# Conditioning and gate rows in four column groups of TensorE, three tiles in the first round, and moved loads, in a one-core layer kernel

## The chip, the cores and the metric

One core of one Trainium2 chip runs the whole kernel. The metric is the device time of one execution in microseconds (us). In the trace PE is TensorE (matrix products), DVE is VectorE, ACT is ScalarE, POOL is GpSimd, and SP is SyncE, which here only issues DMAs. A DMA is issued by the engine whose queue it stands in (SP, ACT or POOL) and lands later by itself. An engine carries out its own instructions in order.

## The reference

One layer of a hybrid backbone for 256 prompt tokens and 2048 latent tokens, D_MODEL = 1024, all in float32:

```python
shift, scale, gate = jnp.split(jax.nn.silu(cond) @ w_mod + b_mod, 3, axis=-1)
xm = _rmsnorm(x, norm_g) * (1.0 + scale[:, None]) + shift[:, None]
(q, k, v, g_na, u, g_lru, c_b, c_c, c_h, g_conv,
 m_na, m_lru, m_conv) = jnp.split(xm @ w_in, SPLIT_IDX, axis=-1)
...
merged = (jax.nn.sigmoid(m_na) * ((o_na * jax.nn.silu(g_na)) @ w_br_na)
          + jax.nn.sigmoid(m_lru) * (((h_f + h_b) * jax.nn.silu(g_lru)) @ w_br_lru)
          + jax.nn.sigmoid(m_conv) * ((o_conv * jax.nn.silu(g_conv)) @ w_br_conv))
x = x + gate[:, None] * (merged @ w_out)
```

o_na is attention with 8 heads of 64: the prompt attends to itself, and each latent token to a window of its 32 x 64 grid (with a bias per head) and to 256 cached keys, in one softmax. h_f and h_b come from two gated linear recurrences, o_conv from short convolutions. cond has two rows, one for the prompt and one for the latents. A last RMSNorm gives the outputs; the prompt's keys, values and final states are outputs too.

## The kernel before

Tokens are cut into chunks: chunk 0 is the prompt (256 tokens), chunks 1 to 4 are 512 latent tokens each. Phase A (`ORDA`) takes chunks 1, 2, 0, and phase B (`ORDB`) chunks 3 and 4. In each phase the input projection goes through tiles of 128 columns of `w_in`: tile m is loaded by `load_w` (two DMAs `wraw` from SP, split into a high part `whi` on ACT and a low part `wlo` on POOL, both rounded), and `w_in_chunk` (L153) multiplies it with a chunk of the normalised input, which is split likewise (`xh`, `xl`). Each product is three passes (high by high, low by high, high by low) over 8 blocks of 128 rows, so one tile of a 512-token chunk is 24 matmuls of 512 columns. `dense` runs a list of such tiles over the chunks of its phase; a `Side` is a generator that `dense` ticks at a given rate, so that recurrences, gate rows and attention stand between the matmuls of the projection. The order of instructions on each engine comes out of this program order and of when buffers of the tile pools come free; a scheduler fixes it before the run.

What the change touches, in program order:

- **Conditioning** (L249 to L269). In eight steps kk a DMA from SP brings 128 rows of `w_mod` (1 MB, tiles `wmxhB`, `wmxlB`, `wm`), and four float32 matmuls (L254) with two weight columns (`sc`, the two conditioning rows) and 512 moving columns add into four PSUM banks `pm`. Then rows 0 and 1 of each bank are copied (`mrow`), transposed (`pmt`, L265) and made into `shft` and `amod`, which the first normalised chunk needs.
- **First round.** Tiles 16 and 17 run over the chunks while the next chunk is prepared.
- **Gate rows** (`gate_rows`, L382 to L399). The last 1024 columns of `w_mod`, needed only at the very end, in 16 float32 matmuls (L396) that stand one by one between projection tiles, each behind its own 256 KB load `wg` (two buffers).
- **Keys of the prompt** (`key_out`, L346). Each of four key tiles is copied by ACT (`kc`, L376) and transposed (`ktr`); the last pair of transposes stands right behind the last product of its tile.
- **Attention** (`latent_steps`, `latent_units`). For phase A group 0, for phase B groups 1, 2 and 3 of each head: jobs (g, h). POOL's queue issues the loads: keys `kd` and `ck` and values `vb` per head, queries `qs` (512 KB) and gate `sg` per job, and the bias `bt` per head and kind (kind 1 serves groups 1 and 2, kind 2 serves group 3; two buffers). PE computes scores `sc` and `sl` (L583, L587), DVE adds `bt` and takes the maximum (L590), ACT exponentiates, DVE normalises (`p`, L598), PE transposes `p` (`t`, L613) and multiplies with the values (`o`, L628). `p_first` is the `p` of the first block of phase B.
- **Branch products** (L922 to L946). For each chunk and branch the operand `zr` is loaded (SP, L927), split into `zh` and `zl`, and multiplied with branch weights into `pb` (L937); the results are scaled by `tg` (the tanh values that tiles 40 to 63 stored in `d_sig`), added on POOL (L944) and stored to `d_mrg` by ACT's queue.
- **Output projection** (from L950). `mr` loads merged rows from `d_mrg` (L958), which are split into `mh` and `ml` and multiplied into `po` (L986). The first 128 rows are already there (`m0h`, `m0l`).

## Time and profile before

| what | before |
|---|---|
| runs | 2567.19, 2556.35, 2554.89 us; median 2556.35 us |
| the profiled execution | 2558.7 us, span 2556.9 us |
| PE busy | 2492.1 us (97% of the span), 13192 records |
| DVE, ACT, POOL busy | 43%, 38%, 34% |
| mean granted clock of PE | 0.989 |
| DMA | 360.84 MB, mean 141 GB/s |

The profiled execution lies 2.3 us above the median of the runs, and 1.8 us of it lie outside the span. PE is busy nearly throughout; the other engines and the DMA matter where PE waits for them.

### The profile page before, as it was taken

What the parts mean: (1) busy time and instruction counts of PE and PEld (TensorE: products, weight loads), DVE (VectorE), ACT (ScalarE), POOL (GpSimd) and SP (SyncE); (2) the same over time, 40 slices, a digit from 0 to 9 for tenths busy, and PEclk for the clock granted to TensorE, in tenths of its full rate; (3) what the DMA queues carried; (4) which work ended last, traced back from release to release, by engine and by line L of the source; (5) the groups of instructions that cost most, each with busy time, mean ns of one, the idle gap of its engine ahead of it and who ended that gap; (6) DMA issues with size and microseconds to landing.
All of it is one profiled execution on the core that took longest, in us unless ns stands there. A gap on an engine that the chain in (4) does not pass through costs nothing. (4 is left out here: it accounts for less than half of the span.)

```text
span 2556.9 us, 35325 instructions
## 1 busy us (share of the span) xinstructions
PE 2492.1 (97%) x13192; PEld 2060.1 (81%) x13192; DVE 1096.7 (43%) x2329; ACT 976.5 (38%) x1849; POOL 878.3 (34%) x757
## 2 busy tenths in 40 slices
PE   8999999999999999999999998999999999999998
PEld 3887678888878888888888887778877788888887
DVE  5101244555223332314877873455544144333433
ACT  4311444344223334335766563445544311011221
POOL 2411223233542321332444444333331313335642
PEclk9999999999999999999999999999999999999999
DMA  7335552322743543345553326546552475555542
GB/s 280 110 91 153 160 132 84 75 58 65 185 118 107 155 146 136 101 133 117 185 162 120 118 87 183 170 142 179 170 145 82 148 239 181 181 161 189 176 137 83
DMA packets 248812, 360.84 MB, mean 141 GB/s; under 512 B 88761, under 2 KB 124729, under 8 KB 247617
## 3 DMA queue, kind: packets, MB, share of 16 engines
q1 hardware_dynamic: 147360, 227.20, 29.5%
q0 software_dynamic: 47920, 64.26, 9.0%
q10 hardware_dynamic: 53360, 67.13, 7.9%
q8 instruction: 104, 1.70, 0.3%
q14 instruction: 68, 0.55, 0.1%
HBM read 248.10 MB, written 110.11 MB: 140 GB/s over the span
## 5 line engine op out<-in xcount | busy, mean ns | idle before, releaser
L153 PE MATMUL ps<-xh,whi 128*128 128x512 f32 (+1 forms) x2400 | 899.8, 375 | 0.0
L153 PE MATMUL ps<-xl,whi 128*128 128x512 f32 (+1 forms) x2400 | 889.4, 371 | 2.1 <-DVE xl L56 1.6
L153 PE MATMUL ps<-xh,wlo 128*128 128x512 f32 (+1 forms) x2400 | 888.8, 370 | 0.0
L153 PEld LDWEIGHTS ps<-xh,whi 128*128 128x128 f32 x2400 | 455.9, 190 | 91.9 <-ACT qo L367 5.2
L56 POOL TENSOR_TENSOR wlo<-wraw,whi 128x512 fp32r<-128x512 f32 x240 | 336.2, 1418 | 550.9 <-ACT whi L55 491.3
L153 PEld LDWEIGHTS ps<-xl,whi 128*128 128x128 f32 x2400 | 456.0, 190 | 78.5 <-POOL xl L56 2.5
L153 PEld LDWEIGHTS ps<-xh,wlo 128*128 128x128 f32 x2400 | 455.3, 190 | 77.9
L55 ACT CAST whi<-wraw 128x512 fp32r<-128x512 f32 x240 | 144.9, 616 | 298.8 <-PE ps L153 168.4
L937 PE MATMUL pb<-zh,wbh 128*128 128x512 f32 (+1 forms) x480 | 179.0, 373 | 4.5 <-ACT zh L55 4.5
L937 PE MATMUL pb<-zl,wbh 128*128 128x512 f32 (+1 forms) x480 | 179.2, 373 | 0.0
L937 PE MATMUL pb<-zh,wbl 128*128 128x512 f32 (+1 forms) x480 | 179.1, 373 | 0.0
L167 ACT ACTIVATE evm<-ps 128x512 f32<-128x512 f32 (+1 forms) x120 | 66.4, 553 | 283.8 <-PE ps L153 282.9
L944 POOL TENSOR_TENSOR tg<-tg,tg 128x512 f32<-128x512 f32 (+1 forms) x80 | 97.0, 1223 | 188.2 <-DVE tg L940 183.4
L588 DVE TENSOR_SCALAR_CACHE_REDUCE p<-sc 128x256 f32<-128x256 f32 x127 | 53.2, 422 | 207.6 <-PE sc L583 206.9
L940 DVE SCALAR_TENSOR_TENSOR tg<-tg,pb 128x512 f32<-128x512 f32 (+1 forms) x120 | 74.9, 631 | 156.5 <-PE pb L937 146.6
L596 ACT ACTIVATE p<-p,ast 128x736 f32<-128x736 f32 (+2 forms) x127 | 109.6, 863 | 41.6 <-DVE ast L595 39.6
L444 DVE SCALAR_TENSOR_TENSOR uf<-ut,pk,uf 128x512 f32<-128x512 f32 (+1 forms) x120 | 104.2, 868 | 31.4 <-ACT uf L441 29.5
L613 PE MATMUL t<-ident,p 128*128 128x128 f32 x698 | 98.7, 275 | 18.9 <-DVE p L598 17.3
L475 POOL TENSOR_TENSOR sq<-sq,ea 128x512 f32<-128x512 f32 (+1 forms) x40 | 61.9, 1549 | 153.5 <-ACT sq L468 94.7
L55 ACT CAST zh<-zr 128x512 fp32r<-128x512 f32 (+1 forms) x60 | 30.5, 575 | 212.3 <-PE pb L937 99.9
L617 ACT COPY pT<-t 128x512 f32<-128x512 f32 (+3 forms) x256 | 95.3, 407 | 37.4 <-PE t L613 37.4
L937 PEld LDWEIGHTS pb<-zh,wbh 128*128 128x128 f32 x480 | 90.8, 189 | 22.3 <-ACT zh L55 5.0
(233 smaller groups left out, 3639.2 us busy)
## 6 DMA issues: line engine op xcount, KB each, us to landing
wraw<-w_in SPq DMA_DIRECT2D x240, 256.0 KB, 3.8
d_sig<-evm ACTq DMA_DIRECT2D x96, 256.0 KB, 4.0
tg<-d_sig SPq DMA_DIRECT2D x96, 256.0 KB, 4.0
xt<-x SPq DMA_DIRECT2D x36, 512.0 KB, 4.2
qs<-d_q POOLq DMA_DIRECT2D x32, 512.0 KB, 17.9
zr<-d_z SPq DMA_DIRECT2D x12, 1024.0 KB, 5.5
d_mrg<-tg ACTq DMA_DIRECT2D x32, 256.0 KB, 4.5
mr<-d_mrg SPq DMA_DIRECT2D x8, 1024.0 KB, 5.8
```

Of the source, the lines that this page charges most:

```text
L55: S.copy(hi, src)
L56: lo_eng.tensor_tensor(lo, src, r2f(hi), ALU.subtract)
L153: TE.matmul(ps[:, :n], (lo if a else hi)[:, k, :], (xl if b else xh)[ci][:, k, :], start=(i == 0), stop=(i == len(ps_) - 1))
L167: S.activation(o[:, :n], ps, AF.Tanh, scale=0.5)
L444: V.scalar_tensor_tensor(uf[:, :n], ut[:, tap : tap + n], cw(tap), uf[:, :n], ALU.mult, ALU.add)
L475: G.tensor_tensor(sq[:, :n], sq[:, :n], ea[:, :n], ALU.mult)
L596: S.activation(p[:, :nk], p[:, :nk], AF.Exp, bias=st[:, 2:3], accum_out=st[:, 3:4])
L613: TE.transpose(tb[:, ti * P : ti * P + P], p[:, c0 : c0 + P], ident)
L617: S.copy(pT[:, base : base + last - first], tb[:, first:last])
L937: TE.matmul(ps[:, :n], (wbl if a_ else wbh)[br * 4 + k][:, m * P : (m + 1) * P], (zl if b_ else zh)[:, k, :n], start=(i == 0), stop=(i == ...
L940: V.scalar_tensor_tensor(t[:, :n], t[:, :n], 1.0, ps[:, :n], ALU.add, ALU.mult)
L944: G.tensor_tensor(acc[m][:, :n], acc[m][:, :n], t[:, :n], ALU.add)
```

## The change

Ten edits. The conditioning uses one PSUM bank with four groups of 32 output partitions in place of four banks. `load_w(18)` and tile 18 join the first round. `gate_rows` has four steps with one 1 MB load `wg` (one buffer) and four matmuls in four column groups each, and adds up two partial sums. One tile with the attention gate, 12, is put ahead of the last key transposes. In attention the bias is loaded ahead of the queries, and in phase B the loads of the next head are called at other steps. Phase B's first loads are called one projection tile earlier in the order (tile 41 goes behind them; the recurrence's rate is 25/74 for 25/76). The pool `xp` is opened ahead of `ep` and `wp`, the last projection tile takes its chunks in reversed order, the pool `wor` stands on the right side of memory, and `zh` and `zl` rotate by name.

```diff
-        pm = [bank(f"pm{i}") for i in range(4)]
+        pm = bank("pm")
...
-                TE.matmul(pm[i][:2, :], sc[:, kk, :], wm[:, i * 512 : (i + 1) * 512],
+                TE.matmul(pm[32 * i : 32 * i + 2, :], sc[:, kk, :], wm[:, i * 512 : (i + 1) * 512],
...
-        wl = [load_w(16), load_w(17)]
+        wl = [load_w(16), load_w(17), load_w(18)]
...
+            w_in_chunk(18, wl[2], ci, u_ev[2])
...
+        pgt = bank("pgt")
+        for kp in range(KD // 2):
+            wg = eq.tile([P, 2, D], F32, tag="wg", name=f"wg{kp}", bufs=1)
+            SY.dma_start(wg, H["w_mod"][256 * kp : 256 * kp + 256, 2048:3072].rearrange("(a p) c -> p a c", p=P))
...
+            for i in range(4):
+                a, hf = i // 2, i % 2
+                TE.matmul(pgt[32 * i : 32 * i + 2, :], sc[:, 2 * kp + a, :], wg[:, a, 512 * hf : 512 * hf + 512],
+                          start=(kp == 0), stop=(kp == KD // 2 - 1))
...
-            for kk in range(KD + 1):
-                if kk < KD:
-                    wg = eq.tile([P, 512], F32, tag="wg", name=f"wg{hf}_{kk}", bufs=2)
-                    SY.dma_start(wg, H["w_mod"][kk * P : (kk + 1) * P, 2048 + 512 * hf : 2560 + 512 * hf])
...
+        def load_group(g, h):
+            bi = GR[g][3]
+            load_bias(g, h)
+            qs = at.tile([P, 2, 512], F32R, tag="qs", name=f"qs{g}_{h}",
...
+                    if nxt and b == 0:
+                        load_group(*nxt)
+                        if g == gs[0]:
+                            load_bias(gs[-1], h)
+                    if h + 1 < HEADS and b == 2:
+                        if g == gs[0]:
+                            load_head(h + 1)
+                        elif g == gs[1]:
+                            load_values(h + 1)
...
+        dense([(12, ev_silu(d_gna, 0))], ORDA, lru)
         while deferred:
             key_out(eq, *deferred.pop(0))
-        dense([(12 + j, ev_silu(d_gna, j)) for j in range(4)], ORDA, lru)
+        dense([(12 + j, ev_silu(d_gna, j)) for j in (1, 2, 3)], ORDA, lru)
...
-        dense([(40 + m, ev_tanh(d_sig, m)) for m in range(2)], ORDB, lru)
+        dense([(40, ev_tanh(d_sig, 0))], ORDB, lru)
...
-        dense([(40 + m, ev_tanh(d_sig, m)) for m in (2, 3)], ORDB)
+        dense([(40 + m, ev_tanh(d_sig, m)) for m in (1, 2, 3)], ORDB)
...
-        dense([(40 + m, ev_tanh(d_sig, m))], ORDB)
+        dense([(40 + m, ev_tanh(d_sig, m))], ORDB if m < 23 else ORDB[::-1])
...
-    wor = es.enter_context(tc.tile_pool(name="wor", bufs=1, reuse_waits="tile"))
+    wor = wbs.enter_context(tc.tile_pool(name="wor", bufs=1, side="right", reuse_waits="tile"))
...
-                zh = zp.tile([P, 4, 512], F32R, tag="zh", name=f"zh{c}_{br}", bufs=3)
+                zi = (3 * c + 2 - br) % 3
+                zh = zp.tile([P, 4, 512], F32R, tag=f"zh{zi}", name=f"zh{c}_{br}", bufs=1)
```

Three places show what this does to the order of instructions.

On PE, at the last two pairs of key transposes before (the numbers behind `ps`, `whi` and `xh` tell tiles apart; a `ps_0` is a product of the prompt's chunk):

```order
L153 MATMUL ps_2_2731<-xh_352,wlo_2689 128x512
L346 MATMUL ktr<-ident,kc 128x128 x2
L153 MATMUL ps_0_2771<-xh_506,whi_2688 128x256
...
L153 MATMUL ps_0_2771<-xh_506,wlo_2689 128x256
L346 MATMUL ktr<-ident,kc 128x128 x2
L153 MATMUL ps_1_2823<-xh_222,whi_2813 128x512
```

And the same two pairs on PE now:

```order
L153 MATMUL ps_2_2705<-xh_359,wlo_2663 128x512
L348 MATMUL ktr<-ident,kc 128x128 x2
L153 MATMUL ps_0_2745<-xh_541,whi_2662 128x256
...
L153 MATMUL ps_0_2903<-xh_541,wlo_2781 128x256
L348 MATMUL ktr<-ident,kc 128x128 x2
L153 MATMUL ps_1_2950<-xh_229,whi_2940 128x512
```

Before, the last pair stands behind `ps_0` of its own tile (weights 2688). Now it stands behind `ps_0` of the next tile (weights 2780), which is one whole tile later.

On POOL, in phase B's attention around the bias of head 3 before (`bt1_3` is kind 1 of head 3, `qs2_3` the queries of group 2 of head 3, `kd4_3` its keys):

```order
L721 DMA ck4_3_14857<-d_ck_59 128x256
L733 DMA qs3_2_14682<-d_q_57 128x2x512
L739 DMA sg2_2_14526<-d_gna_62 64x512
L736 DMA bt2_2_14684<-bias2 128x3x384
L719 DMA kd4_3_14855<-d_k_58 128x1792
...
L733 DMA qs1_3_14859<-d_q_57 128x2x512
L733 DMA qs2_3_15019<-d_q_57 128x2x512
L739 DMA sg1_3_14863<-d_gna_62 64x512
L736 DMA bt1_3_14861<-bias1 128x1440
```

The same stretch of POOL now:

```order
L728 DMA ck4_3_14597<-d_ck_59 128x256
L726 DMA kd4_3_14595<-d_k_58 128x1792
L750 DMA sg2_2_14500<-d_gna_62 64x512
L740 DMA bt2_2_14502<-bias2 128x3x384
L748 DMA qs3_2_14662<-d_q_57 128x2x512
...
L748 DMA qs1_3_14837<-d_q_57 128x2x512
L748 DMA qs2_3_14993<-d_q_57 128x2x512
L750 DMA sg1_3_14839<-d_gna_62 64x512
L740 DMA bt1_3_14835<-bias1 128x1440
```

`kd4_3` has moved ahead of `sg2_2` and `bt2_2`, and `qs3_2` behind them; `bt1_3` stands at the end of the stretch, behind `qs2_3` and `sg1_3`, in both.

On SP, where the branch products begin, before (`wbraw` is a piece of the branch weights, `tg0_2_0` a tile of tanh values):

```order
L886 DMA wbraw3_0_18127<-w_br 128x512
L886 DMA wbraw3_1_18131<-w_br 128x512
L927 DMA zr0_2_18146<-d_z_66 128x4x256
L933 DMA tg0_2_0_18158<-d_sig_67 128x256
L933 DMA tg0_2_1_18174<-d_sig_67 128x256
```

And on SP now:

```order
L908 DMA wbraw3_1_18105<-w_br 128x512
L936 DMA woraw0_20044<-w_out 128x1024
L936 DMA woraw1_20050<-w_out 128x1024
L952 DMA zr0_2_18120<-d_z_66 128x4x256
L958 DMA tg0_2_0_18132<-d_sig_67 128x256
```

Two loads of output weights now stand ahead of the first branch operand `zr0_2`; they came later before. Through the pools' places in memory, `zr0_2` waited before for the last matmul of the last projection tile and now waits for the last matmul of that tile's first chunk; and `mr` of rows 128 to 255 waited before for an early branch product and now waits for the stores of the last two rows of tiles to `d_mrg`.

## Rows read from the trace of the kernel before

**Rows 1.** The page, part 1: busy us, share of the span, instructions of each engine.

```profile
PE 2492.1 (97%) x13192; PEld 2060.1 (81%) x13192; DVE 1096.7 (43%) x2329; ACT 976.5 (38%) x1849; POOL 878.3 (34%) x757
```

**Rows 2.** Waits of PE: line, releaser: us in total, times, longest.

```profile
PE t L613 <- DVE p L598: 17.3, 10, 4.0
...
PE pgt L396 <- DMA wg<-w_mod: 2.2, 1, 2.2
```

**Rows 3.** Timeline of PE, 0 to 42 us: start, us, operation, [idle before].

```profile
21.91 13.90 PE L254 MATMUL pm<-wm,sc 128*2 128x512 f32 x32
35.73 0.90 PE L265 MATMUL pmt<-ident,mrow 2*128 2x2 f32 x12
...
40.52 0.47 PE L153 MATMUL ps<-xh,whi 128*128 128x512 f32 x1
```

**Rows 4.** Tile wm, 0 to 50 us: the loads of the last four steps.

```profile
L252 SPq DMA_DIRECT2D wm<-w_mod x4: 327/328/328, 6.6 to 14.1; - x4
...
DMA to landing us min/median/max: 15.0/15.1/15.1
```

**Rows 5.** Timeline of PE, 1936 to 1950 us, without the projection.

```profile
1943.73 0.82 PE L613 MATMUL t<-ident,p 128*128 128x128 f32 x6
1944.48 0.66 PE L628 MATMUL o<-pT,vb 128*64 128x128 f32 x8
1944.97 0.61 PE L628 MATMUL o<-pT,cv 128*64 128x128 f32 x8
1945.41 0.40 PE L628 MATMUL o<-pT,vb 128*64 128x64 f32 x8
```

**Rows 6.** Timeline of PE, 236 to 245 us: one gate matmul, two records.

```profile
238.00 0.39 PE L153 MATMUL ps<-xh,wlo 128*128 128x512 f32 x1
238.32 1.02 PE L396 MATMUL pgt<-wg,sc 128*2 128x512 f32 x2
239.27 0.50 PE L153 MATMUL ps<-xh,whi 128*128 128x512 f32 x1
```

**Rows 7.** Timeline of PE, 350 to 364 us: the last key transposes.

```profile
351.85 0.28 PE L153 MATMUL ps<-xh,wlo 128*128 128x256 f32 x1
356.30 0.69 PE L346 MATMUL ktr<-ident,kc 128*128 128x128 f32 x2 [4.17 <-ACT kc L376]
...
360.20 0.63 PE L153 MATMUL ps<-xh,wlo 128*128 128x512 f32 x1
360.62 0.63 PE L153 MATMUL ps<-xh,whi 128*128 128x512 f32 x1
```

**Rows 8.** Timelines of POOL and PE where phase B's attention begins.

```profile
1573.43 2.11 POOL L733 DMA_DIRECT2D qs<-d_q  x1
...
1585.20 0.39 PE L153 MATMUL ps<-xh,wlo 128*128 128x512 f32 x1
1594.99 0.77 PE L583 MATMUL sc<-ck,qs 128*128 128x256 f32 x2 [9.40 <-DMA qs<-d_q]
...
1601.30 1.51 PE L613 MATMUL t<-ident,p_first 128*128 128x128 f32 x6 [2.29 <-DVE p_first L598]
```

**Rows 9.** Timelines of POOL and DVE: a late bias in phase B.

```profile
1628.26 0.57 POOL L736 DMA_DIRECT2D bt<-bias  x1
...
1644.55 0.72 DVE L590 CUSTOM_DVE_ANT_0 p<-sl,bt,ast 128x480 f32<-128x480 f32 x1 [4.10 <-DMA bt<-bias]
```

**Rows 10.** Timelines of SP and PE where the branch products begin.

```profile
2041.97 0.38 SPq L927 DMA_DIRECT2D zr<-d_z  x1
...
2046.70 0.51 PE L937 MATMUL pb<-zh,wbh 128*128 128x256 f32 x2 [4.54 <-ACT zh L55]
```

**Rows 11.** Timelines of SP and DVE, and the chain that ended last: the output projection begins.

```profile
2343.70 0.37 SPq L958 DMA_DIRECT2D mr<-d_mrg  x1
...
2350.26 197.79 PE po L986 x864
...
2357.31 0.69 DVE L988 TENSOR_TENSOR y<-po,gb 128x512 f32<-128x512 f32 x1 [1.25 <-DMA d_mrg<-tg]
```

More of the change, by code (lines that the diff above doesn't have):

```diff
@@ L261, in build @@
             mr_ = p0.tile([P, 512], F32, tag="tm", name=f"mrow{i}", bufs=3)
-            (V.tensor_copy if i % 2 else S.copy)(mr_[:2, :], pm[i][:2, :])
+            (V.tensor_copy if i % 2 else S.copy)(mr_[:2, :], pm[32 * i : 32 * i + 2, :])
             for j in range(4):
@@ L271, in build @@
         V.tensor_tensor(amod, amod, pk[:, C_NG : C_NG + 8].unsqueeze(2).broadcast_to([P, 8, 2]), ALU.mult)
-        u_ev = [ev_copy(d_u, j) for j in range(2)]
+        u_ev = [ev_copy(d_u, j) for j in range(3)]
         prep(p0, ORDA[0], xts[ORDA[0]])
@@ L387, in gate_rows @@
             SY.dma_start(bg[:2, :], H["b_gate"][:, hs].broadcast_to([2, 512]))
-            pgt = bank(f"pgt{hf}")
-            nxt = []
-            for kk in range(KD + 1):
-                if kk < KD:
-                    wg = eq.tile([P, 512], F32, tag="wg", name=f"wg{hf}_{kk}", bufs=2)
-                    SY.dma_start(wg, H["w_mod"][kk * P : (kk + 1) * P, 2048 + 512 * hf : 2560 + 512 * hf])
-                    nxt.append(wg)
-                if kk:
-                    TE.matmul(pgt[:2, :], sc[:, kk - 1, :], nxt.pop(0), start=(kk == 1), stop=(kk == KD))
-                yield
-            V.tensor_tensor(bg[:2, :], pgt[:2, :], bg[:2, :], ALU.add)
+            for a in (0, 1):
+                i = 2 * a + hf
+                V.tensor_tensor(bg[:2, :], pgt[32 * i : 32 * i + 2, :], bg[:2, :], ALU.add)
             SY.dma_start(d_gate[:, hs], bg[:2, :])
@@ L727, in load_values, with load_bias @@
             heads[h][2] = vb
-        def load_group(g, h):
+        def load_bias(g, h):
             _, _, nrow, bi = GR[g]
-            qs = at.tile([P, 2, 512], F32R, tag="qs", name=f"qs{g}_{h}",
-                         bufs=3 if len(gs) > 1 else 2)
-            G.dma_start(r2f(qs), twice(h, 256 + 512 * g, 512))
             if (bi, h) not in bias:
@@ L737, in load_group @@
                 bias[bi, h] = bt
+        def load_group(g, h):
+            bi = GR[g][3]
+            load_bias(g, h)
+            qs = at.tile([P, 2, 512], F32R, tag="qs", name=f"qs{g}_{h}",
+                         bufs=3 if len(gs) > 1 else 2)
+            G.dma_start(r2f(qs), twice(h, 256 + 512 * g, 512))
             sg = at.tile([HD, 512], F32, tag="sg", name=f"sg{g}_{h}", bufs=3)
@@ L748, in first_loads, with latent_units @@
             load_values(0)
-        return first_loads, latent_units(at, jobs, heads, groups, cv, row0, load_head, load_group, load_values)
-    def latent_units(at, jobs, heads, groups, cv, row0, load_head, load_group, load_values):
+        return first_loads, latent_units(at, gs, jobs, heads, groups, cv, row0, load_head, load_group, load_values, load_bias)
+    def latent_units(at, gs, jobs, heads, groups, cv, row0, load_head, load_group, load_values, load_bias):
         for ji, (g, h) in enumerate(jobs):
@@ L788, in latent_units @@
                      fin if b == 3 else None)
-                if nxt and b == 0:
-                    if nxt[1] != h:
+                if len(gs) == 1:
+                    if nxt and b == 0:
                         load_head(nxt[1])
-                    load_group(*nxt)
-                if nxt and b == 3:
-                    if nxt[1] != h:
+                        load_group(*nxt)
+                    if nxt and b == 3:
                         load_values(nxt[1])
+                else:
+                    if nxt and b == 0:
+                        load_group(*nxt)
+                        if g == gs[0]:
[5 more added lines that the diff above has]
+                            load_values(h + 1)
                 yield
@@ L801, in chain @@
             yield from g
-    dense([(16 + j, ev_copy(d_u, j)) for j in (2, 3)] +
+    dense([(19, ev_copy(d_u, 3))] +
           [(20 + j, ev_silu(d_glru, j)) for j in range(4)], ORDA)
@@ L924, in build @@
                 zr = zp.tile([P, 4, 512], F32, tag="zraw", name=f"zr{c}_{br}", bufs=1)
-                zh = zp.tile([P, 4, 512], F32R, tag="zh", name=f"zh{c}_{br}", bufs=3)
-                zl = zp.tile([P, 4, 512], F32R, tag="zl", name=f"zl{c}_{br}", bufs=3)
+                zi = (3 * c + 2 - br) % 3
+                zh = zp.tile([P, 4, 512], F32R, tag=f"zh{zi}", name=f"zh{c}_{br}", bufs=1)
+                zl = zp.tile([P, 4, 512], F32R, tag=f"zl{zi}", name=f"zl{c}_{br}", bufs=1)
                 SY.dma_start(zr[:, :, :n], d_z[br * 512 : (br + 1) * 512, cs].rearrange("(k p) t -> p k t", p=P))
```

8 lines of the change are left out of this document (6 added, 2 removed).

## The prediction

> **What bounds the kernel now.** I read the page's busy times first. PE works for 2492.1 of 2556.9 us [rows 1], so only about 65 us of PE standing still can be won, plus PE work that is taken out and stretches in which PE runs at half its granted clock. The list of PE's waits came second: 17.3 us go to the softmax result `p` in ten waits, 2.2 us to a gate load [rows 2], and single long ones stand in the timelines: 4.17 us before a pair of key transposes [rows 7], 9.40 and 2.29 us where phase B's attention begins [rows 8], 4.54 us where the branch products begin [rows 10]. The timelines show what such a wait costs behind it. After the 4.17 us wait, matmuls of 512 columns start 0.42 us apart (360.20, 360.62) [rows 7], against 0.229 us in the output projection (197.79 us for 864) [rows 11]; so for a while PE is on the lower of its two clock levels. The ten matmuls between the transposes of 356.30 and the one at 360.62 lose some 0.2 us each, which makes a short dip worth about 2 us. Any gain must be one of these.
>
> The sum is made against the profiled execution, 2558.7 us, which lies 2.3 us above the median of the runs; I carry the difference over to the median, 2556.35. Half a per cent, 12.8 us, is about what a measurement of this kernel can tell from no change.
>
> **Column groups: what one is worth.** The last 16 conditioning matmuls (32 records, as each float32 matmul has two) take from 21.91 to 35.73, 13.82 us or 0.432 us per record of 512 columns [rows 3]. A record of 128 columns would take a quarter, 0.108 us. The attention's value products have 128 columns and already go in turn to two groups of 64 output partitions: 16 records take from 1944.48 to 1945.41, 0.058 us each [rows 5]. Two groups are thus 1.86 times as fast as one. For four groups no row exists. Lower bound: one, if they queue; upper: four. I take two, because the two records of an instruction use the same group and must follow each other, and PE takes instructions in order: then only the second record of one and the first of the next lie beside each other, however many groups there are (four instructions take 5 record times in place of 8).
>
> The Trainium skill (TensorE: Matmul & The Clock Gate, Part 3) says that matmuls in different column groups run side by side, and gives 2.38 for three tiles; its model would make four nearly as quick as one. No run here shows that for float32. By it the gate rows below would gain about 14 us and not 9; this is a rival.
>
> Against the change speaks another rule (TensorEngine Tiling (Array Packing), Key Properties): a change of tiling mode drains TensorE. The row shows six transposes from 1943.73 and the first grouped product at 1944.48 [rows 5], 0.75 us; at 0.11 us a transpose, 0.09 us are left. By the trace a switch is therefore at most 0.1 us, and eight switches 0.8 us.
>
> **The sum, part by part.**
>
> *Conditioning.* The loads of the last steps are issued up to 14.1 us and land 15.1 us later, at 29.2 [rows 4]. PE's last conditioning matmul ends at 35.73, and the projection starts at 40.52 [rows 3]. At two, the last step needs 5 × 0.432 = 2.2 us behind its load, so it ends near 31.4: the loads are the new limit. What follows (copies, transposes, `amod`, the first normalised block) took 4.8 us. In the new order more input transposes stand ahead of the last `pmt`, so I take 5.5. The start is at 36.9: 3.6 us gained. Bounds: 0 (groups queue, or the clock is low while PE waits for loads) to 6 (the whole end falls to the load).
>
> *Three tiles in the first round.* The same 24 matmuls per chunk; I found no wait of PE behind the first 52 us that they could fill or open. 0, cover being weights loaded two tiles ahead; bounds -1 to +2.
>
> *Gate rows.* One gate matmul pushes its neighbours 1.27 us apart (238.00 to 239.27) where 0.23 would do [rows 6, 11]: 1.04, and with the switch to and from it about 1.15. Sixteen cost 18.4 us. Now four sets of 5 × 0.432 + 0.2 = 2.4 us, 9.5 us. That is 8.9 gained, and most of the 2.2 us wait for a load [rows 2], because the 1 MB loads have about 20 us of projection between sets: 10 in all. Bounds 3.5 (one) to 15 (four).
>
> *Key transposes.* The last pair waits 4.17 us for ACT's copy and is followed by a dip of 2 us [rows 7]. One whole tile later the copy is long done; the next in line is the projection's next matmul, whose weights are there. 6.3 gained; bounds 4.2 to 6.5.
>
> *First loads of phase B.* PE's last projection matmul starts at 1585.20, the scores wait for `qs` until 1594.99 (issued 1573.43, so some 21.5 us before), and the first transposes start at 1601.30 [rows 8]: 15.9 us from 1585.43, where that matmul's 0.23 us are over. One more tile, two chunks of 24 × 0.229 = 11.0 us, now stands between the last recurrence matmul and the scores, so loads start 11.0 us earlier in PE's time. `qs` is now issued behind `bt`, whose 0.74 MB (128 × 1440 × 4 bytes) at twice the mean DMA rate of 141 GB/s are an estimate of 2.6 us. The 9.4 us wait for `qs` falls to about 1.2 us. From the first score to the transposes it took 6.3 us, partly on the lower clock; at the higher I take 4.6, of which 2.3 stay idle as before. The first transposes then follow 5.8 us behind the last tile, not 15.9. 10 gained; bounds 6 (loads slowed by the extra traffic) to 15 (no wait and no dip).
>
> *Loads in the steady part of phase B.* `bt` of the next head is issued at 1628.26 and DVE goes on with it 16.3 us later, after 4.10 us of waiting [rows 9]; this is how most of the 17.3 us on `p` [rows 2] come about. By the order, this load stays where it is, behind `qs` of group 2, because its buffer is freed only then. Only `kd` and `qs` of group 3 change places, and that `qs` has a whole job in hand. 0; bounds -4 to +6.
>
> *Branch operand.* `zr` was issued at 2041.97 and PE began at 2046.70 after 4.54 us of waiting [rows 10], with a dip behind it. The last tile now runs chunk 4 first and chunk 3 last, and `zr` waits for chunk 4's matmuls alone, which end 5.5 us (24 × 0.229) before PE ends the tile. From issue to PE's start, load and first split took 4.73 us, which fits into that; what is late next is the second `zr`, which PE needs a whole branch later. 6.3 gained; bounds 4 to 6.5 (two loads of output weights go ahead of it on SP).
>
> *A new wait.* `mr` of rows 128 to 255 was issued at 2343.70, long before `po` starts at 2350.26. Now it must wait for the last stores to `d_mrg`, the last of which landed at 2357.31, when DVE was released [rows 11]: 7.1 us into `po`. A load of like size and its first split took 4.7 us [rows 10], which makes 11.8; PE needs it after 48 matmuls, 11.0 us. So PE waits about 1 us, and SP, which holds `gb`, `fg` and the next `mr` behind it, passes its delay on: the results `y`, which wait for `gb`, and the next rows come some 7 us later than before. No row shows how much of that the buffers take up; I take half of it. That makes -4.5; bounds -1 (the buffers take all) to -8 (none).
>
> Sum: 3.6 + 0 + 10 + 6.3 + 10 + 0 + 6.3 - 4.5 = 31.7 us. 2558.7 - 31.7 = 2527.0 for the profiled execution, 2556.35 - 31.7 = 2524.7 against the median.
>
> **The rivals.**
>
> *Groups don't overlap.* Then the gate rows give 3.5 and the start nothing: 31.7 - 6.5 - 3.6 = 21.6, 2535. For it speaks that no row has four groups; against it rows 5, where two do overlap.
>
> *Four groups run as one, and the biases come early.* The gate rows give 15, the start 4.5, and phase B 6 more: 31.7 + 5 + 0.9 + 6 = 43.6, 2513. With overlap alone, 2519. Rows 5 can't tell it from the forecast, since with two groups both make two; against it speak the two records of an instruction, which share a group.
>
> *Little is won where phase B's attention begins.* If the earlier loads meet the last traffic of the recurrence and `qs` lands only 4 us earlier in PE's time, that term is 4, and the sum 25.7: 2531.
>
> *Slower: the bias becomes later.* Place: the wait of DVE on `bt` at each of seven head changes. Each us that `bt` lands later there is a us of PE, since that wait is already exposed by 4.10 us [rows 9]. If `bt` were issued behind one more job (about 14 us), 7 × 14 = 98 us would be lost: 2623. It decides for slower from (31.7 + 12.8) / 7 = 6.4 us per head on. Against it stands the order, where `bt1_3` keeps its place; for it, that `kd` (0.9 MB, 128 × 1792 × 4 bytes) is now further ahead in the same queue.
>
> **Chances.** The forecast 0.5; groups that don't overlap 0.13; four as one 0.2; nothing won at phase B's start 0.13; slower 0.04. The likeliest gives 2525 us. The range takes the overlap rival's lower side with no new wait, 2513 - 4 = 2508 (rounded), and on the upper side serial groups with the phase B term at its lower bound and the new wait at 8: 2535 + 4 + 3.5, 2543. Faster by over 0.5% (below 2543.6) has 0.86: the first four cases without their tails; same 0.10: several terms at their lower bounds at once; slower 0.04.
>
> **What the changed profile would show.** Column groups: four gate matmuls (eight records) that push their neighbours 2.2 to 2.6 us apart, not 4.4 (one) or 1.2 (four); the first projection matmul near 36.9. Keys, operand: no wait on `kc` and none on `zh`. Phase B: a wait for `qs` under 3 us, and the waits on `p` still near 17 us. Output: a PE wait on `mh` or `ml` of rows 128 to 255 of 1 to 4 us near the start of `po`. I am wrong if the groups queue or fully overlap, if `qs` still comes 9 us late, or if the output projection loses more than 8 us.

## The result, and the profile after

| what | before | after |
|---|---|---|
| median | 2558.49 us | 2544.61 us |
| all six runs | 2552.97 to 2567.19 us | 2538.20 to 2546.65 us |
| ratio, 95% interval | 1 | 0.9939 [0.9926, 0.9953] |
| the profiled execution, span | 2558.7, 2556.9 us | 2546.65, 2544.8 us |

The change makes the kernel 13.9 us faster, 0.6%. The forecast was a gain of 31.7 us, to 2525, in a range up to 2543: the sign was right, the size less than half, and the time lies just outside the range.

First the page of the changed kernel, busy times:

```profile
PE 2466.8 (97%) x13192; PEld 2056.4 (81%) x13192; DVE 1100.3 (43%) x2331; ACT 976.1 (38%) x1849; POOL 877.5 (34%) x757
```

PE's busy time fell by 25 us [rows 1], the span by 12: part of what PE no longer does, it now waits. The list of PE's waits after (us in total, times, longest):

```profile
PE t L620 <- DVE p L605: 19.2, 13, 4.3
PE scp L590 <- DMA kp<-d_k: 9.2, 4, 3.8
PE pm L255 <- DMA wm<-w_mod: 8.4, 4, 6.6
PE pm L255 <- DMA wmxhB<-w_mod: 7.0, 2, 6.5
...
PE ktr L348 <- ACT kc L378: 3.4, 2, 2.4
PE ps L153 <- ACT whi L55: 3.0, 1, 3.0
PE t L620 <- DVE p_first L605: 2.4, 1, 2.4
PE sc L590 <- DMA qs<-d_q: 2.2, 1, 2.2
...
PE pb L962 <- ACT zh L55: 1.5, 1, 1.5
```

Against [rows 2] the gate load has gone from the list, the waits for `qs` and `zh` are down to 2.2 and 1.5 us, and those on `p` are 19.2 us against 17.3. Three things are new or longer: PE waits for the loads of the conditioning (6.5 of the 7.0 us on `wmxhB` are the wait for the first load, which before has too), a wait of 3.0 us for a weight cast `whi`, and four for `kp`, the keys of the prompt's attention, 9.2 us against 4.3.

To place gain and loss I made a ledger of both traces: at a given time, the time passed minus the usual start-to-start spacing of all PE instructions started until then (0.23 us for a product of 512 columns, and so on for each form; conditioning and gate matmuls count nothing). What is left is the time that PE has lost. It is worked out from all PE records; the table gives what it grew by in each stretch, after minus before, so a gain is negative.

| stretch of the span, us | what happens there | forecast | measured |
|---|---|---|---|
| 0 to 200 | conditioning, first tiles | -3.6 | -2.3 |
| 200 to 330 | gate rows | -10 | -15.1 |
| 330 to 400 | last key transposes | -6.3 | -4.0 |
| 680 to 1000 | prompt's attention (`kp`) | 0 | +4.2 |
| 1200 to 1250 | a weight cast, late | 0 | +6.8 |
| 1570 to 1620 | first loads of phase B | -10 | -5.9 |
| 1620 to 2000 | steady part of phase B | 0 | +8.6 |
| 2000 to 2100 | first branch operand | -6.3 | -4.7 |
| 2100 to the end | output projection | +4.5 | +0.5 |

These rows sum to -11.9 (the spans differ by 12.1). They are of one profile each; in kernels with the same code in a stretch they differ by 2 to 4 us, with `kp` by some 6 and in the steady part of phase B by up to 8 (below). A row of that size can't be put down to an edit by itself.

**Gate rows.** PE's timeline after, around one set:

```profile
233.28 0.39 PE L153 MATMUL ps<-xh,wlo 128*128 128x512 f32 x1
233.60 1.04 PE L396 MATMUL pgt<-wg,sc 128*2 128x512 f32 x8
234.57 0.50 PE L153 MATMUL ps<-xh,whi 128*128 128x512 f32 x1
```

Four matmuls (eight records) push their neighbours 1.29 us apart, where 0.23 would do: 1.06. Before, a single one cost 1.04 [rows 6]. Four groups are 3.9 times as fast as one, and no wait for `wg` is left. Each of the four matmuls has two records: the trace has the four first records starting within 0.02 us of each other, and the four second ones 0.43 us behind them.

**Start.** PE's timeline after, and windows of 4 us (busy time and records of PE, PEld, DVE, ACT, POOL, then granted clock, DMA share, GB/s), two of after and then one of before:

```profile
21.43 1.89 PE L255 MATMUL pm<-wm,sc 128*2 128x512 f32 x8 [6.55 <-DMA wm<-w_mod]
...
28.95 1.47 PE L255 MATMUL pm<-wm,sc 128*2 128x512 f32 x8 [0.62 <-DMA wm<-w_mod]
38.42 0.50 PE L153 MATMUL ps<-xh,whi 128*128 128x512 f32 x1 [1.73 <-ACT xh L55]
40.84 0.80 PE L153 MATMUL ps<-xl,whi 128*128 128x512 f32 x1 [1.92 <-DVE xl L56]
```

```profile
16.00:20.00 4.00, 0.00 (x0) 0.00 (x0) 0.00 (x0) 3.56 (x8) 0.00 (x0) 0.53 1.04 422
24.00:28.00 4.00, 3.39 (x16) 0.16 (x16) 1.43 (x3) 0.00 (x0) 0.00 (x0) 0.50 0.99 408
```

```profile
24.00:28.00 4.00, 4.00 (x11) 0.85 (x10) 1.67 (x3) 0.00 (x0) 0.00 (x0) 1.00 1.00 415
```

The last conditioning matmul ends at 30.4, 5.3 us earlier than before [rows 3]. The projection starts only 2.1 earlier: it waits for the normalised input, `xh` from ACT and `xl` from DVE. And PE, after standing 6.55 us in front of the fifth step's load, is on the lower clock level (0.50 is 1.2 GHz), where before, busy throughout, it had 1.00.

**The late cast.** PE's one line, then ACT's rows ahead of it:

```profile
1224.67 0.79 PE L153 MATMUL ps<-xh,whi 128*128 128x512 f32 x1 [2.96 <-ACT whi L55]
```

```profile
1215.49 1.28 ACT L464 ACT_TABLE_LOAD   x1
...
1220.91 1.28 ACT L475 ACT_TABLE_LOAD   x1
...
1222.83 0.80 ACT L448 ACTIVATE uf<-ut,pk 128x512 f32<-128x512 f32 x1
1224.01 0.61 ACT L55 CAST whi<-wraw 128x512 fp32r<-128x512 f32 x1
```

A step of phase B's recurrence, with its table loads, stands ahead of the cast on ACT. PE waits 2.96 us and then runs on the lower clock up to 1231.

**Phase B's start.** PE after, then POOL, then the waits of SP's queue from 1570 to 1600 (us in total, times, longest), then ACT (`evm` is the tanh that ACT makes of a product `ps`, `pT` ACT's copy of the transposed `p`):

```profile
1577.53 0.47 PE L590 MATMUL sc<-ck,qs 128*128 128x256 f32 x2 [2.25 <-DMA qs<-d_q]
...
1582.22 0.84 PE L620 MATMUL t<-ident,p_first 128*128 128x128 f32 x6 [2.40 <-DVE p_first L605]
...
1594.09 0.43 PE L635 MATMUL o<-pT,vb 128*64 128x128 f32 x2 [1.30 <-ACT evm L167]
...
1596.95 0.90 PE L635 MATMUL o<-pT,vb 128*64 128x128 f32 x5 [1.55 <-ACT pT L624]
```

```profile
1562.90 0.54 POOL L726 DMA_DIRECT2D kd<-d_k  x1 [2.83 <-DMA bt<-bias]
1577.68 0.56 POOL L728 DMA_DIRECT2D ck<-d_ck  x1 [14.24 <-DMA qs<-d_q]
...
1583.03 5.00 POOL L56 TENSOR_TENSOR wlo<-wraw,whi 128x512 fp32r<-128x512 f32 x4
```

```profile
SPq L143 <- POOL wlo L56: 40.2, 6, 32.7
```

```profile
1592.92 0.62 ACT L55 CAST whi<-wraw 128x512 fp32r<-128x512 f32 x1 [8.88 <-DMA wraw<-w_in]
```

The 9.40 us wait for `qs` [rows 8] is down to 2.25. But now the second bias and the second head's keys are issued while the first loads are still under way. POOL stands 14.24 us in front of `ck` until a `qs` has landed, and the weight splits `wlo` queued behind it start at 1583. SP's next weight loads `wraw` wait for these splits and go out from 1584.36 on. On ACT the cast of the next weights waits 8.88 us for `wraw`, with `evm` queued behind it, and PE meets two short waits, for `evm` and `pT`, with slower products behind them.

**Steady part.** DVE's row for the next bias:

```profile
1628.96 0.72 DVE L597 CUSTOM_DVE_ANT_0 p<-sl,bt,ast 128x480 f32<-128x480 f32 x1 [4.35 <-DMA bt<-bias]
```

As forecast, this load still lands late: 4.35 us of waiting against 4.10 [rows 9]. In all, DVE waits 15.3 us for `bt` there, before 18.8.

**Branch operand and output.** SP's load of the first branch operand, PE's first branch product, and the loads `mr` between 2320 and 2360 (ns min/median/max, first and last start):

```profile
2029.01 0.38 SPq L952 DMA_DIRECT2D zr<-d_z  x1
...
2035.91 0.50 PE L962 MATMUL pb<-zh,wbh 128*128 128x256 f32 x2 [1.49 <-ACT zh L55]
```

```profile
L983 SPq DMA_DIRECT2D mr<-d_mrg x3: 370/590/764, 2342.5 to 2356.7; - x3
```

The 4.54 us in [rows 10] are 1.49: from the issue of `zr` to PE's start it took 6.9 us. `mr` is issued 4.8 us behind the first product of `po` (2337.7), where before it was issued ahead of it [rows 11]; PE has no wait on `mh` or `ml` there.

### The profile page after: what moved, and what is told of

It reads as the page before. It is cut to its first block, busy times and chain, and to the rows that moved or that the text cites. A ratio compares the mean times of both kernels' runs of the same rounds, so it can differ in the third digit from the quotient of the medians.

```text
span 2544.8 us, 35298 instructions
## 1 busy us (share of the span) xinstructions
PE 2466.8 (97%) x13192; PEld 2056.4 (81%) x13192; DVE 1100.3 (43%) x2331; ACT 976.1 (38%) x1849; POOL 877.5 (34%) x757
## 5 line engine op out<-in xcount | busy, mean ns | idle before, releaser
L620 PE MATMUL t<-ident,p 128*128 128x128 f32 x698 | 100.9, 279 | 22.9 <-DVE p L605 19.2
L620 PEld LDWEIGHTS t<-ident,p 128*128 128x128 f32 x698 | 83.6, 143 | 36.8 <-DVE p L605 21.9
```

What stands on the lines that cost most here:

```text
L620: TE.transpose(tb[:, ti * P : ti * P + P], p[:, c0 : c0 + P], ident)
```

## The experiments

The kernel before, run beside them on the same chip, had medians of 2559.3, 2560.8 and 2559.7 us for the first, second and third four. Ratios are to it. After means the changed kernel; its 2544.61 was taken beside a kernel before of 2558.49 us, so differences to it carry some 2 us of that spread.

**Gate rows alone** (e1): before, with `gate_rows` of after.

```diff
+            for i in range(4):
+                a, hf = i // 2, i % 2
+                TE.matmul(pgt[32 * i : 32 * i + 2, :], sc[:, 2 * kp + a, :], wg[:, a, 512 * hf : 512 * hf + 512],
```

> The kernel before with one edit: gate rows in four steps of four matmuls in four column groups, one 1 MB load each. Theory (four groups run side by side, as the gate rows of the changed kernel suggest, 1.04 us for four matmuls): each set pushes its neighbours about 1.3 us apart, the sixteen matmuls cost 4.3 us and not 16.6, the 2.25 us wait for a gate load goes, and the time falls by 14 to 15 us, to about 2543.5. Rival 1 (two records of an instruction follow each other, so two-fold): sets of 2.4 us, gain 10, about 2548. Rival 2 (the gain is given back at the next exposed wait, the key transposes or the prompt's key loads): the sets are short but the time falls by under 9 us, and the waits of PE on kc or kp are longer than 4.2 and 4.3 us.

2551.48 us, 0.9972 [0.9962, 0.9982]. The ledger has 13.3 us gained at 330 us and 8.0 at 400: the key transposes take 5.3 back. The waits for `kc` in this kernel, and the last pair:

```profile
PE ktr L346 <- ACT kc L376: 9.2, 3, 4.8
```

```profile
348.21 0.69 PE L346 MATMUL ktr<-ident,kc 128*128 128x128 f32 x2 [4.84 <-ACT kc L376]
```

9.2 us in three waits where before had 4.2 in one: PE comes to the keys sooner, and ACT's copies don't keep up.

**Gate rows and keys** (e6): e1 with tile 12 ahead of the last transposes.

```diff
+        dense([(12, ev_silu(d_gna, 0))], ORDA, lru)
         while deferred:
             key_out(eq, *deferred.pop(0))
```

> The kernel before with two edits: gate rows in column groups, and tile 12 ahead of the last key transposes. Theory (shorter gate rows bring PE to the key transposes earlier than ACT's copies, so the gate rows alone were paid back there; with a tile between, the copies are done): PE's waits on kc fall from the 9.2 us of the gate rows alone to under 4, the stretch up to 400 us is 18 to 21 us shorter than before (8 with the gate rows alone), and the time is 2543 to 2547, some 6 us under the gate rows alone; the rest is given back at the prompt's key loads. Rival (ACT is behind anyway and the wait moves to the next pair): waits on kc stay at 8 us or more, and the time stays at 2551.

2543.3 us, 0.9941 [0.9925, 0.9958], a gain of 17.5 where the gate rows alone gave 7.8. The ledger has 17 us gained at 400 us, a little under the 18 to 21 expected. These two edits give as much as the whole change. What the others win and lose comes to nothing, and there the search goes on.

```profile
PE ktr L346 <- ACT kc L376: 3.4, 2, 2.4
```

The last pair no longer waits; an earlier pair does, 2.4 us.

**Conditioning alone** (e2): one bank and four groups, nothing else.

```diff
-        pm = [bank(f"pm{i}") for i in range(4)]
+        pm = bank("pm")
...
+                TE.matmul(pm[32 * i : 32 * i + 2, :], sc[:, kk, :], wm[:, i * 512 : (i + 1) * 512],
```

> The kernel before with one edit: the conditioning matmuls in four column groups of one bank. Theory (the loads of the conditioning weights become the limit, and PE, which stands still between them, runs on the lower clock when the projection starts): the last conditioning matmul ends near 30.5 us, the first projection matmul starts near 38, the first dozen of projection matmuls start 0.43 us apart, and the gain is 2 to 3 us: about 2556. Rival (the prediction's 3.6 and more: only the landing of the last load matters and the clock costs nothing): the gain is 4 us or more and the first projection matmuls are on the higher clock.

2560.3 us, 1.0006 [0.9993, 1.0018]: nothing.

```profile
29.16 1.87 PE L254 MATMUL pm<-wm,sc 128*2 128x512 f32 x8 [0.64 <-DMA wm<-w_mod]
38.00 0.50 PE L153 MATMUL ps<-xh,whi 128*128 128x512 f32 x1 [0.70 <-ACT xh L55]
```

The conditioning ends at 31.0 and the projection starts at 38.0, both early; by 200 us the ledger shows no gain left, but some 3 us lost behind the start. In the other kernels with the four groups the start lies anywhere from 38.4 to 41.3.

**Conditioning with PE kept busy** (e8): e4 (below) with a second set of the same matmuls into a bank that nothing reads, to hold the clock up.

```diff
+            for i in range(4):
+                TE.matmul(pf[32 * i : 32 * i + 2, :], sc[:, kk, :], wm[:, i * 512 : (i + 1) * 512],
```

> The changed kernel with three bias buffers and a second set of the same conditioning matmuls into an unused bank behind each step, so that PE works about 2.1 of 2.5 us while it waits for the conditioning weights. Theory (what the conditioning gains, it loses because PE, idle most of that time, goes to the lower clock, and the transposes and first projection matmuls run there): the granted clock stays at 1.0 between 24 and 40 us, the first projection matmul starts near 38 us and not 41.3, and the time falls by 2 to 4 us against the kernel with three bias buffers (2528.3), to about 2525. Rival (DVE, ACT and POOL, which make the normalised input, are the limit between 38 and 52 us): the clock stays up but the stretch up to 100 us is the same within 1 us, and so is the time.

2527.35 us, 0.9873 [0.9855, 0.9890], within 1 us of e4 (2528.33). A window of e4 and its first product, then the same of e8:

```profile
32.00:36.00 4.00, 4.00 (x21) 3.42 (x21) 1.22 (x2) 3.51 (x7) 3.59 (x3) 0.50 0.57 145
...
41.30 0.78 PE L153 MATMUL ps<-xh,whi 128*128 128x512 f32 x1
```

```profile
32.00:36.00 4.00, 4.00 (x39) 3.26 (x35) 1.37 (x2) 3.76 (x8) 4.00 (x4) 1.00 0.43 118
...
39.48 0.51 PE L153 MATMUL ps<-xh,whi 128*128 128x512 f32 x1 [1.78 <-ACT xh L55]
```

From 32 to 36 PE now does 39 records where e4 did 21, and its first product starts 1.8 us sooner. In e4 that product waited for nothing but PE's own transposes on the lower clock; in e8 it waits for `xh`. The start of all kernels with the four groups goes by the granted clock from 32 to 40: at 1.00 it lies between 38.0 and 39.5 (after, e2, e8, e9, e10), at 0.50 between 39.5 and 41.3 (e3, e4, e5, e7, e11, e12). So the clock does hold the start in some kernels. Little of it is left at the end: from 40 to 44 the clock falls in e8 too (0.70), and the runs of e4 and e8 overlap.

**The recurrence's rate** (e3): after with 25/76.

```diff
-        lru = Side(lru_steps(lp, True), 25 / 74)
+        lru = Side(lru_steps(lp, True), 25 / 76)
```

> The changed kernel with one number set back: phase B's recurrence is ticked at 25/76 of the projection tiles, not 25/74. Theory (the new stall of PE near 1221 us, 3.0 us of waiting for a weight cast and a dip behind it, comes from the recurrence step that stands ahead of that cast on ACT one tile earlier than before): the stall is gone or under 1 us, and the time falls by 4 to 7 us against the changed kernel, to about 2539 (2544.6 less 5.5); what is left of the recurrence at its end costs up to 2 us near 1570. Rival (the stall comes from another edit, or only from that one execution): a wait of PE for whi of about 3 us near 1221 stays, or is absent in a kernel of the same time, and the time stays within 2 us of the changed kernel.

2543.84 us, 0.9941 [0.9928, 0.9955], as after. The late cast is gone, no wait of PE stands between 1200 and 1260, and the ledger is 4.6 us ahead at 1570. It is lost again where phase B starts; POOL's row, then PE's:

```profile
1554.90 0.53 POOL L740 DMA_DIRECT2D bt<-bias  x1 [5.86 <-DMA d_z<-hf]
...
1579.22 0.77 PE L590 MATMUL sc<-ck,qs 128*128 128x256 f32 x2 [8.54 <-DMA qs<-d_q]
...
1589.62 1.51 PE L620 MATMUL t<-ident,p_first 128*128 128x128 f32 x6 [6.69 <-DVE ast L604]
```

POOL stands 5.86 us in front of the first bias until the recurrence's last store (`d_z<-hf`) has landed; in the changed kernel it doesn't. PE, 4.6 us ahead, then waits 8.54 us for the queries behind it. So 25/74, which makes the late cast, is also what brings phase B's first loads early.

**Three bias buffers** (e4): after, with a third `bt` in phase B.

```diff
-                bt = at.tile([P, 3, nrow_max * 32], F32, tag="bt", name=f"bt{bi}_{h}")
+                bt = at.tile([P, 3, nrow_max * 32], F32, tag="bt", name=f"bt{bi}_{h}",
+                             bufs=3 if len(gs) > 1 else 2)
```

> The changed kernel with three buffers for the bias in phase B in place of two. Theory (the bias of the next head is issued late because its buffer is freed late, and it then lands 16 us later behind the queries of 0.5 MB in the same queue, so moving the call earlier in the source changed nothing): with a free buffer it is issued a job or more earlier; DVE's waits for the bias and PE's long waits on p (3 to 4.3 us each at the changes of head) go, PE's total on p falls from 19.2 to under 8 us, and the time falls by 12 to 20 us against the changed kernel, to about 2528. Rival (the queue itself is the limit: whatever is issued earlier makes the queries or keys late): DVE's waits move to other tiles or PE waits for qs, and the time stays within 4 us of the changed kernel's 2544.6.

2528.33 us, 0.9879 [0.9864, 0.9895]: 16.3 us under after. The waits on `p`:

```profile
PE t L620 <- DVE p L605: 6.5, 10, 1.3
```

19.2 us have become 6.5, and DVE never waits for `bt` (15.3 us in after). The free buffer, not the call, is what makes the load early: e9 (below) has the third buffer with the old calls.

**Fourth `sp` buffer and 25/72** (e7): e4 with both.

```diff
-            sp = pp.tile([HD, 256], F32, tag="sp", name=f"sp{h}", bufs=3)
+            sp = pp.tile([HD, 256], F32, tag="sp", name=f"sp{h}", bufs=4)
...
+        lru = Side(lru_steps(lp, True), 25 / 72)
```

> The changed kernel with three bias buffers and two more edits at places far apart: four buffers for the prompt's gate tile sp (the load of sp waits on POOL's queue for a store two heads back, and the next keys kp stand behind it), and a recurrence rate of 25/72 in phase B. Theory: PE's waits on kp fall from 8.0 to under 4 us with their dips, worth 4 to 7 us between 690 and 800 us; no wait for whi of over 1 us near 1221 to 1230 us and none in its place, worth 5 to 6: together 2517 to 2520. Rival 1 (kp waits for its own buffer or lands late in traffic, not for sp): waits on kp stay at 6 us or more. Rival 2 (the recurrence meets another weight cast at this rate): a wait of PE for whi of 2 us or more stands elsewhere between 1150 and 1580 us.

2533.77 us, 0.9900 [0.9883, 0.9916]: 5.4 us over e4.

```profile
PE scp L590 <- DMA kp<-d_k: 11.9, 3, 7.8
...
PE ps L153 <- ACT whi L55: 3.0, 1, 3.0
```

The `kp` waits are longer, 11.9 us against 8.0 in e4, so nothing speaks for a lack of `sp` buffers; in the ledger the whole loss lies there. And the late cast has only moved on: PE stands from 1233 to 1236.

**The loads of before** (e5): after with the order and the call places of attention loads as they were, the rest of the change kept.

```diff
-            load_bias(g, h)
             qs = at.tile([P, 2, 512], F32R, tag="qs", name=f"qs{g}_{h}",
...
-                        if g == gs[0]:
-                            load_bias(gs[-1], h)
-                    if h + 1 < HEADS and b == 2:
-                        if g == gs[0]:
-                            load_head(h + 1)
...
+                if nxt and b == 0:
+                    if nxt[1] != h:
+                        load_head(nxt[1])
+                    load_group(*nxt)
```

> The changed kernel with the order of attention loads set back (queries ahead of the bias, keys and values of the next head called with its first job). Theory (the new order is inert in the steady part of phase B; the 8.6 us that the changed kernel's profile lost there against the one of before is the spread of the bias waits from execution to execution, as in the gate-rows-only run, which lost 4.8 there with the old code): the time is within 4 us of the changed kernel's 2544.6, and PE's waits on p stay at 15 to 20 us. Rival (keys and bias of kind 2 ahead of the queries make the later bias later): the waits on p fall by 3 us or more and the time falls by 6 us or more, to under 2539.

2530.01 us, 0.9887 [0.9869, 0.9904]: 14.6 us faster than after. The theory, that the new order is inert, was wrong; the rival has the time, but not the place: the waits on `p` are 17.5 us, 1.7 under after. The new order of attention's loads is what eats the gain. POOL at phase B's start:

```profile
1571.14 0.78 POOL L750 DMA_DIRECT2D bt<-bias  x1 [11.54 <-DMA qs<-d_q]
...
1574.56 2.51 POOL L56 TENSOR_TENSOR wlo<-wraw,whi 128x512 fp32r<-128x512 f32 x2
...
1579.79 2.54 POOL L56 TENSOR_TENSOR wlo<-wraw,whi 128x512 fp32r<-128x512 f32 x2
```

POOL waits here too, but earlier, and the four splits are done by 1582.3, not 1588.0; PE meets neither the wait for `evm` nor that for `pT`. The stretch 1570 to 1620 loses 4.2 us of PE (after 9.6, before 15.4), the steady part 18.0 (after 25.1, before 16.5). The waits on `kp`, which also are shorter here (6.3 against 9.2), vary from kernel to kernel and may be some of the 14.6.

**The two halves of it**: queries ahead of the bias, new call places (e11); old call places, bias ahead (e12). Their diffs are the first and the last part of the one above.

> The changed kernel with one part of the load order set back: queries ahead of the bias, while keys, values and second bias keep their new calls. Theory (of the 14.6 us that the whole old order brings, about half are lost where phase B's attention begins, where the bias ahead delays the first queries): PE's wait for the first queries falls from 2.2 us to under 1, the stretch from 1570 to 1620 us loses 3 to 5 us and not 10, and the time is 2536 to 2540. Rival (the calls for keys and second bias do it all): the time stays at 2542 to 2546.

> The changed kernel with the other part set back: keys, values and biases called at the old steps, while the bias stays ahead of the queries of its own job. Theory (the rest of the 14.6 us is lost because keys of 0.9 MB and the second bias are in the queue ahead of the queries that follow): PE's waits on p and ast fall from 22.7 to about 18 us, the steady part from 1620 to 2000 us loses 16 to 20 us and not 25, and the time is 2536 to 2540. Rival (the steady part only spreads from execution to execution): the steady part still loses 21 to 25 us, and the time stays at 2542 to 2546.

e11 2545.11 us, 0.9947 [0.9933, 0.9961], no better than after; e12 2535.86, 0.9908 [0.9890, 0.9926], 8.7 under it. By the ledger the call places decide phase B's start: with the old ones it loses 1.6 (e12) and 4.2 (e5), with the new ones 10.0 (e11) and 9.6 (after). With queries first but the new calls (e11), POOL still stands in front of the next head's keys; in e12 the first two of its splits are early again:

```profile
1576.45 0.56 POOL L726 DMA_DIRECT2D kd<-d_k  x1 [14.23 <-DMA qs<-d_q]
```

```profile
1579.25 2.52 POOL L56 TENSOR_TENSOR wlo<-wraw,whi 128x512 fp32r<-128x512 f32 x2
```

Both expectations had the places the other way round. In these four kernels the steady part goes by the order within a group: 18.0 with queries first (e11, e5), 24.7 and 25.1 with the bias first (e12, after). Other kernels blur that (13.5 to 21.3 with queries first in before, e1, e2 and e6, 21.0 with the bias first in e3), e12's profile is of a run 5.8 us above its median, and the halves don't add up to e5's 14.6: in medians the order within a group is worth 5.9 us with the old calls (e5 against e12) and nothing with the new ones (e11 against after).

**Loads of before and three bias buffers** (e9), the edits of e5 and e4.

> The changed kernel with the old order of attention loads and three bias buffers. Theory (the new load order costs some 14 us at phase B's start and in its steady part; the late bias costs another 15 in any order, because its buffer is freed late): the two gains add up, PE's waits on p fall from 17.5 to about 6 us, and the time falls from the 2530.0 of the old order to about 2516. Rival (both touch the same waits): 2525 to 2529, as with either edit alone.

2515.65 us, 0.9825 [0.9812, 0.9839], 14.4 under e5. The two repairs add almost in full (14.6 and 16.3 apart, 29.0 together), and the third buffer is worth as much with the old calls as with the new.

**Fill and phase** (e10): e9 with the second conditioning set of e8, and the recurrence started a little later at nearly the old rate.

```diff
+        lru = Side(lru_steps(lp, True), 25.25 / 74)
+        lru.due = -0.2
```

> The kernel with the old load order and three bias buffers, and besides the second set of conditioning matmuls, and a recurrence in phase B that runs at 25.25/74 from -0.2, so that its early steps come one projection tile later (as at 25/76) and its last one still comes ahead of the end. Theory (the stall near 1221 us depends on which tile a recurrence step meets): no wait for whi of over 1 us near 1221, the stretch from 1200 to 1250 us loses under 1 us (6.6 before), and the time is 5 to 9 us under the kernel without these two edits: about 2509. Rival (the stall only moves): a wait for whi of 2 us or more elsewhere, and a time within 3 us of that kernel.

2510.18 us, 0.9809 [0.9794, 0.9824]: 49.5 us under before and the fastest of all. The longest of PE's waits:

```profile
PE scp L594 <- DMA kp<-d_k: 6.8, 4, 3.5
```

No wait for `whi` ahead of a `ps` is left in its list: the late cast, 5.6 us in e9's ledger, is absent, and it is about what e10 gains on e9 (5.5); the second conditioning set is not told apart in it.

## Why the prediction was right and wrong

**What failed: the order of attention's loads in phase B.** Two steps read it as harmless: for the steady part, "Only `kd` and `qs` of group 3 change places, and that `qs` has a whole job in hand", 0 us; for the start, 10 us from loads that are issued 11 us earlier. I followed the one load that DVE waits for, and it did not come later: DVE's waits for `bt` are 15.3 us against 18.8. I didn't follow what shares POOL with it: the weight splits `wlo`, which stand behind every DMA that POOL can't yet issue. At the start the wait for `qs` did shrink nearly as worked out (2.25 where I had 1.2), and from there to the transposes it took 4.7 us where I had 4.6. Then the extra loads held POOL for 14.24 us, POOL's splits held SP's weight loads, and these the cast on ACT: 5.9 of the 10 us came. e5 shows the price of the whole order, 14.6 us in medians, and that the earlier first loads alone are worth the forecast: with the old order phase B's start gains 11.2 us on before. With the loads as they were, the change would have come to 2530, within the forecast's range. That it is the call places at the start is shown by e12 (8.7 us in medians) and POOL's rows. For the steady part it is not shown: e5 against e12 points to the bias ahead of the queries, with some 6 us, e11 against after to nothing, and the 8.6 us in the table are hardly more than kernels with the same code differ by there.

**A term that was missing: the recurrence's rate.** The diff has 25/74 for 25/76, and I gave it no price. It puts a recurrence step ahead of a weight cast on ACT: 6.8 us. e3 takes the stall away by the rate alone; e10 too, with another phase. The rate was not all loss: the term for the first loads rests on a recurrence that ends a tile earlier, and e3, without that, lost at phase B's start what it had saved.

**Mis-sized: gate rows**, 15.1 us where I had 10 (15 was my upper bound), so the rival of four groups as one was right in this. The premise that "the two records of an instruction use the same group and must follow each other" holds: the second ones start 0.43 us behind. What I drew from it is wrong, that only the second record of one matmul and the first of the next lie beside each other: all four first records start together, and eight records in four groups take the time of two in one. Besides, the 1.04 us between neighbours already held the switch of groups, which I added again (1.15). The Trainium skill (TensorE: Matmul & The Clock Gate, Part 3) says that matmuls in different column groups run side by side; the trace agrees, for float32 too, with 1.06 us for four against 1.04 for one. But of these 15 us e1 kept 7.8: the key transposes, next in line, gave back 5.3.

**Mis-sized: conditioning**, 3.6 forecast, 2.3 in after's ledger, nothing that e2's median can tell. The loads are the limit, as the text had it; its 5.5 us for what follows are 8.0 in after (30.4 to 38.4), since the first product waits for `xh`. In six of the eleven kernels with four groups the transposes ahead of it ran on the lower clock, which the prediction had only in its lower bound.

**Key transposes**: the pair's wait went, and 4.0 of 6.3 us came. I asked what is late next and named the projection; it was another pair of transposes, 2.4 us. Behind the shorter gate rows the same edit was worth more, 9.7 us (e6 against e1). **Branch operand**: 4.7 of 6.3, since load and first split took 6.9 us and not 4.73, and `zh` is still 1.49 us late. **Switches**: a set of gate matmuls costs 1.06 us where two record times are 0.86, so there and back they cost 0.2 at most, as forecast. **Three tiles**: not tried alone. Between 52 and 100 us the ledger loses 0.1 to 3.3 us in the four kernels with two tiles (before, e1, e2, e6) and at most 0.3 in the others, so the third tile may be worth something.

**The new wait** was priced at 4.5 us and cost 0.5. `mr` is issued behind the start of `po`, but 4.8 us behind it and not 7.1, and PE never waits in the output projection. My half-way choice had no row behind it; the lower bound of 1 was right.

**`kp`**: the 4.2 us lost between 680 and 1000 can't be put down to an edit. The one edit near it is the order of bias and queries in phase A's attention, and it doesn't divide the kernels: the waits on `kp` are 4.2 to 9.2 us in all with the bias first (after, e3, e4, e8, e12) and 4.3 to 9.3 with the queries first (before, e1, e2, e5, e6, e9, e10, e11). What decides it stays open; a fourth `sp` buffer (e7) didn't shorten it.

Sum of the errors, measured minus forecast, in the order of the table: 1.3 - 5.1 + 2.3 + 4.2 + 6.8 + 4.1 + 8.6 + 1.6 - 4.0 = 19.8 us, which is 31.7 - 11.9.

## What to carry to other kernels

When loads are moved in a queue whose engine also computes, follow that engine's arithmetic and not only the load: here a DMA that had to wait held four weight splits and with them the next weight loads, and undoing the calls alone gave 8.7 us, the whole order 14.6, more than the change as a whole. A load can't be made earlier than its buffer: calling the bias early left PE's waits on `p` where they were (19.2 us, in e5 17.5), and a third buffer gave 16.3 us with the early calls and 14.4 with the old ones. Price every number in the diff, a rate of 25/74 for 25/76 too: it decides which instructions meet, and when the loads behind them may start.

## What the runs showed of the hardware

- Four float32 matmuls of two weight columns in four column groups took 1.06 us of PE's time, one had taken 1.04. Their four first records started within 0.02 us of each other, the second ones 0.43 us behind.
- The same matmuls in the conditioning got ahead of their loads: PE stood 6.55 us in front of the fifth step's load and 0.6 us in front of each later one, and the granted clock was 0.53 from 16 to 20 us and 0.50 from 24 to 28, where before, busy throughout, it had 1.00. In e4 PE stood 5.7 us at that place, and the clock fell only behind 28 us. Where the clock was at 0.50 from 32 to 40 us, the transposes there ran at 21 or 22 records in 4 us in place of 37 to 39, and the first product started up to 3 us later.
- POOL stood 14.24 us in front of a DMA it was to issue until an earlier 512 KB load had landed, with arithmetic queued behind it; in e5 11.54 us, at a place where less depended on it.
- A wait of 2.96 us on PE cost 6.8, since the products behind it ran on the lower clock for some 6 us (0.43 us apart). The other seven kernels with this wait lost 5.6 to 7.1 us there.
